# First values, keys and queries of a two-block layer side by side by k-tile, with squares by token and moving operands at multiples of 64 bytes

## The chip, the core and the metric

The kernel runs on one core of one Trainium2 chip. The metric is the device time of one execution in microseconds; three executions of the kernel before took 1695.17, 1696.14 and 1696.08 us, median 1696.08 us. A time is called "the same" here when it lies within 0.2% of the one before, about 3.4 us.

## The reference, cut

Two transformer blocks run one after the other on 256 tokens of 2048 features, all in float32. The change lies at the start of the first block; its second part (where tiles lie) touches all of both.

```python
def rmsnorm(x, g):
    y = xf * lax.rsqrt(jnp.mean(xf * xf, axis=-1, keepdims=True) + EPS)
    return (y * g.astype(jnp.float32)).astype(x.dtype)

def first_block(x, ...):
    h = rmsnorm(x, pre_mix_g[l])
    proj = h @ w_in[l]
    q_a, k_a, v_a, q_b, k_b, v_b, f_b = jnp.split(proj, cuts, axis=-1)
    o_a = swa_sink_attention(q_a, k_a, v_a, sinks[l])            # 16 heads of 64, 2 kv heads
    log_f = jax.nn.log_sigmoid(f_b + b_forget[l])
    o_b = forgetting_attention(q_b, k_b, v_b, log_f)             # 16 heads of 64
    mix = concat([rmsnorm(o_a), rmsnorm(o_b)]) @ w_out[l]
    x = x + rmsnorm(mix, post_mix_g[l])
    u = causal_dwconv(rmsnorm(x, pre_ffn_g[l]) @ w_up[l], ...)   # 2 x 5632 columns
    x = x + rmsnorm((gelu(gate) * val) @ w_down[l], post_ffn_g[l])
# then second_block(x, mem, ...): the products w_in_2, w_out_2, w_xq, w_xkv, w_xo
```

## The kernel before

Every projection is a product over 2048 features, that is 16 k-tiles of 128 (w_down has 44). Both operands are split into two float32r parts whose sum is the float32 value, so a product is three matmuls: high by high, high by low, low by high. Weights are loaded as raw blocks `wr` (4 buffers, on SyncE's queue, L76), the high part `wh` is made on ScalarE (L92), the low part `wl` on VectorE (L99), 3 buffers each.

A product has one of two forms. In **ws_sub** weights are stationary and the activations move: for each k-tile and each of two tiles of 128 output columns there is a pair, `wl` against 256 columns (L227) and `wh` against 512 columns (L228), the 512 being both parts of 256 tokens next to each other; the pair of the first k-tile stands at L224 and L225. An output group of 256 columns has 32 pairs at 16 k-tiles. In **as_chunk** activations are stationary and 388 to 414 columns of weights move, six matmuls per k-tile (L256 to L258).

TensorE, VectorE, ScalarE and GpSimd run in the order in which Python emits the work: projections are the main line, and generators (attention, norms) emit one stage at a time between k-tiles. In the first stage the order is: the 16 k-tiles of x (tile `R`) are loaded and split into tiles `X0` to `X3` (L193 on ScalarE, L201 on VectorE); the first chunk of 390 value columns runs over all 16 k-tiles; meanwhile the squares of x are made (two quarters on GpSimd at L530, two on ScalarE at L533), summed on GpSimd (L535, L536, L306), then by a matmul with ones (L292), and `rms` and `by_token` (L294 to L301, L313) give the scale by row (`rb1`, `rq`) and by token (`rb1c`). Then the chunk is evicted (L554), 128 columns of keys follow over all k-tiles, then four groups of windowed queries. The group of the queries called q0 below is the first of them, q1 the second.

A tile has a tag, and the tags' order of first use gives its place in SBUF. The places, read from the built program, as bytes modulo 64 within a partition (a moving operand of a pair starts at its tile's place plus a multiple of 2048 bytes):

```
tiles                                        before   after
X0 to X3  (activations, moving in pairs)       32       0
B3 B4 B7 B8 B9 B10 (the same, other stages)    32       0
B0 B1 B2 B5 B6 (the same)                       0       0
wh, wl (stationary in pairs, moving in chunks) 32      32
```

Before, the B tiles at 0 are all at a multiple of 128. After, X0 to X3, B6 and B7 are at 64 modulo 128, the other B tiles at 0. Of the pairs, 3104 of 3856 have their moving operand at 32 modulo 64 before, none after. In w_down an output group takes its 44 k-tiles in the order B0, B1, ... B10, four k-tiles (8 pairs) to a tile.

## Time and profile before

| what | value |
|---|---|
| median of three runs | 1696.08 us |
| span of the profiled execution | 1693.5 us |
| TensorE busy | 1642.7 us (97%) |
| TensorE weight loads busy | 1428.6 us (84%) |
| VectorE busy | 1133.0 us (67%) |
| ScalarE busy | 947.2 us (56%) |
| GpSimd busy | 390.8 us (23%) |
| mean of the DMA traffic | 178 GB/s |

The profile is of one execution; of it the span from the first to the last instruction is known, which is 2.6 us below the median of the three timed runs. Matmuls are pipelined and their ends are modelled, so "busy" of TensorE counts overlap and its mean per instruction says less than the distance from one start to the next.

### The profile page before, as it was taken

To read this page: it belongs to the slowest core of one execution; us is meant where nothing else is said; L and a number is where in the kernel's file an instruction comes from. 1 tells how busy PE (TensorE), PEld (TensorE's weight loads), DVE (VectorE), ACT (ScalarE), POOL (GpSimd) and SP (SyncE) were. 2 spreads that over 40 slices of the span, in tenths; PEclk is the share of its full clock that TensorE was granted. 3 is DMA by queue.
4 is the path that set the end of the run, shared out by engine and by line. 5 is a ranking of instruction groups with operands and counts; after the bars stand their busy time and mean duration, and the time that the engine had idled before them with its cause. 6 is when DMAs were issued, how large, how long until landed. Compare 5 with 4: busy or idle time off the path is not lost. (4 is left out here: it accounts for less than half of the span.)

```text
span 1693.5 us, 25090 instructions
## 1 busy us (share of the span) xinstructions
PE 1642.7 (97%) x9444; PEld 1428.6 (84%) x9444; DVE 1133.0 (67%) x1592; ACT 947.2 (56%) x1479; POOL 390.8 (23%) x300
## 2 busy tenths in 40 slices
PE   6999999989999999999999999997999999999996
PEld 6888888877888888888888888886989888888895
DVE  7677765788777777777775444468664555666766
ACT  5575566755555555555554444455445665655655
POOL 4434642343221122112210000003210222211112
PEclk9999999999999999999999999999999999999998
DMA  6545554745555555555555555664545544556752
GB/s 227 206 131 168 162 157 137 234 137 172 188 183 192 185 187 184 192 185 187 183 193 187 188 186 190 204 204 131 179 135 170 191 146 158 165 191 205 225 165 103
DMA packets 87465, 301.19 MB, mean 178 GB/s; under 512 B 9792, under 2 KB 9824, under 8 KB 87088
## 3 DMA queue, kind: packets, MB, share of 16 engines
q1 hardware_dynamic: 85968, 294.23, 53.2%
q0 software_dynamic: 1232, 5.08, 0.9%
q8 instruction: 74, 1.21, 0.3%
q14 instruction: 47, 0.39, 0.1%
q10 hardware_dynamic: 144, 0.28, 0.1%
HBM read 296.65 MB, written 2.90 MB: 177 GB/s over the span
## 5 line engine op out<-in xcount | busy, mean ns | idle before, releaser
L99 DVE TENSOR_TENSOR wl<-wr,wh 128x1024 fp32r<-128x1024 f32 (+5 forms) x556 | 709.6, 1278 | 328.7 <-ACT wh L92 327.8
L92 ACT ACTIVATE wh<-wr 128x1024 fp32r<-128x1024 f32 (+5 forms) x556 | 574.9, 1035 | 572.1 <-PE P L228 398.3
L228 PE MATMUL P<-X,wh 128*128 128x512 f32 x1867 | 664.0, 399 | 0.0
L228 PE MATMUL P<-B,wh 128*128 128x512 f32 x1734 | 617.3, 398 | 3.4 <-DVE B L201 3.3
L227 PE MATMUL P<-X,wl 128*128 128x256 f32 x1867 | 529.8, 284 | 1.3 <-ACT wh L92 1.3
L227 PE MATMUL P<-B,wl 128*128 128x256 f32 x1734 | 494.8, 285 | 8.9 <-DVE wl L99 8.9
L228 PEld LDWEIGHTS P<-X,wh 128*128 128x128 f32 x1867 | 352.6, 189 | 81.6
L228 PEld LDWEIGHTS P<-B,wh 128*128 128x128 f32 x1734 | 328.5, 189 | 79.4 <-DVE B L201 4.9
L227 PEld LDWEIGHTS P<-X,wl 128*128 128x128 f32 x1867 | 354.0, 190 | 6.9 <-issue 2.6
L227 PEld LDWEIGHTS P<-B,wl 128*128 128x128 f32 x1734 | 329.5, 190 | 13.6 <-DVE wl L99 10.1
L808 POOL TENSOR_TENSOR e<-e,rb 128x512 f32<-128x512 f32 x44 | 93.3, 2121 | 401.8 <-DVE e L273 395.3
L273 DVE TENSOR_TENSOR e<-P,e 128x512 f32<-128x512 f32 (+1 forms) x96 | 66.1, 688 | 147.1 <-ACT e L272 143.8
L330 POOL TENSOR_TENSOR acc<-acc,tc 128x512 f32<-128x512 f32 x18 | 26.9, 1497 | 274.8 <-ACT tc L329 274.8
L256 PE MATMUL P<-wh,B 128*128 128x412 f32 (+2 forms) x208 | 73.4, 353 | 0.0
L257 PE MATMUL P<-wl,B 128*128 128x412 f32 (+2 forms) x208 | 69.7, 335 | 1.0 <-DVE wl L99 1.0
L258 PE MATMUL P<-wh,B 128*128 128x412 f32 (+2 forms) x208 | 69.7, 335 | 0.0
L813 ACT ACTIVATE tc<-e,cols 128x256 f32<-128x256 f32 x88 | 48.2, 595 | 28.5 <-POOL e L808 28.5
L272 ACT ACTIVATE e<-P 128x512 f32<-128x512 f32 (+1 forms) x96 | 55.3, 577 | 0.0
L256 PE MATMUL P<-wh,X 128*128 128x390 f32 (+2 forms) x112 | 40.0, 357 | 7.4 <-ACT wh L92 7.4
L257 PE MATMUL P<-wl,X 128*128 128x390 f32 (+2 forms) x112 | 38.9, 347 | 6.0 <-DVE wl L99 6.0
L818 DVE SCALAR_TENSOR_TENSOR tc<-e,cols,tc 128x254 f32<-128x254 f32 x88 | 42.5, 483 | 3.1
L224 PE MATMUL P<-X,wh 128*128 128x512 f32 x117 | 43.6, 396 | 0.0
(287 smaller groups left out, 1621.4 us busy)
## 6 DMA issues: line engine op xcount, KB each, us to landing
wr<-w_up SPq DMA_DIRECT2D x176, 512.0 KB, 4.2
wr<-w_down SPq DMA_DIRECT2D x88, 512.0 KB, 4.4
wr<-w_out SPq DMA_DIRECT2D x64, 512.0 KB, 4.5
wr<-w_qkb SPq DMA_DIRECT2D x32, 512.0 KB, 3.9
wr<-w_sb SPq DMA_DIRECT2D x32, 512.0 KB, 4.0
wr<-w_gate SPq DMA_DIRECT2D x32, 512.0 KB, 3.9
wr<-w_v SPq DMA_DIRECT2D x24, 412.0 KB, 3.4
wr<-w_qa SPq DMA_DIRECT2D x16, 512.0 KB, 4.4
```

The lines of the kernel that those rows point to most:

```text
L92: k.nc.scalar.activation(h[:, :n], src, AF.Copy)
L99: self.k.nc.vector.tensor_tensor(out=l[:, :n], in0=src, in1=h[:, :n].bitcast(F32), op=ALU.subtract)
L224: mm(pt[t], h[:, o:o + P], xf, start=True, stop=False)
L227: mm(pt[t][:, 0:S], l[:, o:o + P], xk[:, 0, :], start=False, stop=False)
L228: mm(pt[t], h[:, o:o + P], xf, start=False, stop=last)
L256: mm(o, xh, hh, start=kt == 0, stop=False)
L257: mm(o, xh, ll, start=False, stop=False)
L258: mm(o, xl, hh, start=False, stop=kt == KT - 1)
L272: nc.scalar.activation(e1[:, t0:t1, :], p[:, 0:t1 - t0, S:2 * S], AF.Copy)
L273: nc.vector.tensor_tensor(out=e2[:, t0:t1, :], in0=p[:, 0:t1 - t0, 0:S], in1=e1[:, t0:t1, :], op=ALU.add)
L808: nc.gpsimd.tensor_tensor(out=e, in0=e, in1=self.rb2(self.r2), op=ALU.mult)
L813: nc.scalar.activation(y[:, t, :], e[:, t, :], AF.Identity, scale=w(t, 2), bias=w(t, 3))
```

## The change

Three things are done. **First**, the first 390 value columns, the 128 key columns and the 256 columns of q0 are laid side by side in one weight block per k-tile (`w_first`, 774 columns), and a loop over k-tiles does all three products of a k-tile before the next: 6 matmuls of the chunk, one pair of the keys, two pairs of q0, each into PSUM banks of its own. x is loaded in eight parts, two ahead of the loop and the rest within it, each k-tile is split two k-tiles ahead of its use, and the gains needed for that come in a small load of their own (`gain0`). **Second**, x is loaded a second time with tokens on partitions (`xtok`, two loads of 1 MB into tags B6 and B7), and ScalarE squares it and sums along the row in one instruction per half (`accum_out`). The scale by token comes from [128, 2] operands in `rms_tok`, the scale by row from a matmul of ones with a diagonal (`by_row`). The squares and sums on GpSimd are gone. **Third**, small pads (`pad`) and the new order of first use place the tiles as in the table above. From q1 on TensorE's order is as before, apart from five small transposes and sums of the forget gates, which stood among the keys and q0 and now stand in q1; the forget gates and the attention are started later by the generators' counts (2 and 8 k-tiles after q0).

The diff, cut to its core (the left out hunks remove comments, or rename a tag that nothing here rests on):

```diff
+    def pad(self, n=8):
+        self.uid += 1
+        self.nc.gpsimd.memset(self.sb.tile([P, n], F32, name=f"pad_{self.uid}", tag=f"pad{self.uid}", bufs=1), 0.0)
...
+    def ws_tiles(self, pt, xk, h, l, first, last):
+        mm = self.nc.tensor.matmul
+        xf = xk.rearrange("p a b -> p (a b)")
+        for t, o in enumerate(pt):
+            wh, wl = h[:, t * P:(t + 1) * P], l[:, t * P:(t + 1) * P]
+            if first:
+                mm(o, wh, xf, start=True, stop=False)
+                mm(o[:, 0:S], wl, xk[:, 0, :], start=False, stop=False)
+            else:
+                mm(o[:, 0:S], wl, xk[:, 0, :], start=False, stop=False)
+                mm(o, wh, xf, start=False, stop=last)
...
+    def as_halves(self, ps, xk, hh, ll, kt):
+        mm = self.nc.tensor.matmul
+        for half in range(2):
+            xh, xl = xk[:, 0, half * P:(half + 1) * P], xk[:, 1, half * P:(half + 1) * P]
+            o = ps[:, half, :hh.shape[1]]
+            mm(o, xh, hh, start=kt == 0, stop=False)
+            mm(o, xh, ll, start=False, stop=False)
+            mm(o, xl, hh, start=False, stop=kt == KT - 1)
...
+    def rms_tok(self, ssq, n, tag):
+        nc = self.nc
+        rc = self.t((P, 2), tag)
+        nc.scalar.activation(rc, ssq, AF.Ln, scale=1.0 / n, bias=self.epsc[:, 0:1])
+        nc.scalar.activation(rc, rc, AF.Exp, scale=-0.5)
+        m = self.t((P, 2), "rcm")
+        nc.vector.tensor_scalar(out=m, in0=ssq, scalar1=-0.5 / n, scalar2=-0.5 * EPS, op0=ALU.mult, op1=ALU.add)
+        for _ in range(2):
+            nc.vector.tensor_tensor(out=m, in0=m, in1=rc, op=ALU.mult)
+        nc.vector.scalar_tensor_tensor(out=rc, in0=m, scalar=1.5, in1=rc, op0=ALU.add, op1=ALU.mult)
+        dg = self.t((P, 2, P), "td", bufs=2)
+        for half in range(2):
+            nc.vector.tensor_scalar(out=dg[:, half, :], in0=self.ident, scalar1=rc[:, half:half + 1], scalar2=None,
+                                    op0=ALU.mult)
+        return rc, dg
+    def by_row(self, dg):
+        ps = self.p("O")
+        for half in range(2):
+            self.nc.tensor.matmul(ps[:, half * P:(half + 1) * P], self.ones, dg[:, half, :], start=True, stop=True)
+        return ps[:, 0:S]
...
+        self.gain0 = self.t((P, KT), "gain0")
+        nc.sync.dma_start(self.gain0, a["gain0"])
         nc.scalar.dma_start(self.cols, a["cols"])
         self.ident = self.t((P, P), "ident")
         nc.gpsimd.dma_start(self.ident, a["ident"])
         self.ones = self.t((P, P), "ones")
         nc.gpsimd.memset(self.ones, 1.0)
-        self.mhalf = self.t((P, 2), "mhalf")
-        nc.gpsimd.memset(self.mhalf, -0.5)
...
-        narrow("w_v", 0, V_CHUNKS)
-        wide("w_ka")
+        for i in range(KT):
+            units.append((a["w_first"][i], [FIRST_W]))
         wide("w_qa")
...
+        gain = lambda kt: self.gain0[:, kt:kt + 1]
+        def load(c):
             nc.sync.dma_start(R[:, 2 * c:2 * c + 2, :], a["xT"][:, 2 * c:2 * c + 2, :])
-            if c in (0, 2, 4):
-                self.ws.dma()
-        for kt in range(KT):
-            self.split(x(kt), R[:, kt, :], self.col("pre_mix", kt))
-            if kt in (1, 4, 7):
-                self.ws.split()
-                self.ws.flush()
-        acc = self.t((P, 2, 512), "B10")
-        accf = acc.rearrange("p a b -> p (a b)")
-        def squares():
-            for c in range(4):
-                src = R[:, 4 * c:4 * c + 4, :].rearrange("p a b -> p (a b)")
-                sq = self.t((P, 4 * S), f"B{c + 6}") if c else accf
-                if c < 2:
-                    nc.gpsimd.tensor_tensor(out=sq, in0=src, in1=src, op=ALU.mult)
-                else:
-                    yield 4
-                    nc.scalar.activation(sq, src, AF.Square)
-                if c:
-                    nc.gpsimd.tensor_tensor(out=accf, in0=accf, in1=sq, op=ALU.add)
-            nc.gpsimd.tensor_tensor(out=acc[:, 0, :], in0=acc[:, 0, :], in1=acc[:, 1, :], op=ALU.add)
-            yield 10
-            yield from self.first_norm([self.fold(acc[:, 0, :].rearrange("p (a b) -> p a b", a=2))])
+        for c in range(2):
+            load(c)
+            self.ws.dma()
+            self.ws.dma()
+        xt = [self.t((P, D), tg) for tg in ("B6", "B7")]
+        self.pad()
+        ssq = self.t((P, 2), "ssq")
+        sq = self.t((P, D), "B10")
 
         V = [self.t((P, D), "B3"), self.t((P, D), "B4")]
+        self.pad()
         o = VW + 16
         ka = V[0][:, o:o + S]
         acca = [V[0][:, o + i * S:o + (i + 1) * S] for i in (1, 2)]
         accb = [V[1][:, o + P + i * S:o + P + (i + 1) * S] for i in (0, 1)]
...
-        def v_chunk(ci):
+        def v_evac(ps, ci):
             c0, c1 = V_CHUNKS[ci]
-            if ci == 0:
-                it = self.push(squares())
-            ps = self.as_chunk(x, c1 - c0)
-            if ci == 0:
-                self.drain(it)
             for half in range(2):
                 nc.scalar.activation(V[half][:, c0:c1], ps[:, half, :c1 - c0], AF.Copy, scale=self.rc[:, half:half + 1])
 
-        v_chunk(0)
-        rb, rq = self.rb, self.rq
-        fg = self.push(self.fox_gates(V), 2)
+        def v_chunk(ci):
+            v_evac(self.as_chunk(x, V_CHUNKS[ci][1] - V_CHUNKS[ci][0]), ci)
         va = lambda h, half: V[half][:, (h // 8) * 64:(h // 8) * 64 + 64]
         vb = lambda h, half: V[half][:, 144 + h * 64:144 + h * 64 + 64]
 
-        ps = self.big()
-        for k0 in (0, 8):
-            self.ws_sub(ps, x, list(range(k0, k0 + 8)), (0, KT - 1), 1)
-        self.push(self.scaled(ps, ka.unsqueeze(1), rb))
+        n = V_CHUNKS[0][1]
+        psv, psq, psk = self.big(), self.big(), self.p("S", bufs=2)
+        for kt in range(-2, KT):
+            i = kt + 2
+            if i < KT:
+                self.split(x(i), R[:, i, :], gain(i))
+                if i % 2 and i // 2 + 2 < 8:
+                    load(i // 2 + 2)
+                if i in (8, 10):
+                    nc.sync.dma_start(xt[i // 2 - 4], a["xtok"][:, i // 2 - 4, :])
+            self.ws.split()
+            self.ws.flush()
+            if kt < 0:
+                continue
+            h, l, m = self.ws.get()
+            xk = x(kt)
+            self.as_halves(psv, xk, h[:, :n], l[:, :n], kt)
+            for pt, o in (([psk], n), ([psq[:, t, :] for t in range(2)], n + P)):
+                self.ws_tiles(pt, xk, h[:, o:o + len(pt) * P], l[:, o:o + len(pt) * P], kt == 0, kt == KT - 1)
+            self.ws.done()
+            if kt in (10, 12):
+                half = kt // 2 - 5
+                nc.scalar.activation(sq, xt[half], AF.Square, accum_out=ssq[:, half:half + 1])
+            if kt == 13:
+                self.rc, dg = self.rms_tok(ssq, D, "rb1c")
+        ps = self.by_row(dg)
+        self.rb, self.rq = self.t((P, S), "rb1"), self.t((P, S), "rq")
+        nc.vector.tensor_copy(self.rb, ps)
+        nc.vector.tensor_scalar(out=self.rq, in0=ps, scalar1=0.125, scalar2=None, op0=ALU.mult)
+        rb, rq = self.rb, self.rq
+        v_evac(psv, 0)
+        self.push(self.scaled([psk], ka.unsqueeze(1), rb))
...
-            ps = self.ws_group(x)
+            ps = self.ws_group(x) if g else psq
             self.push(self.scaled(ps, qa[:, 2 * g:2 * g + 2, :], rq, "swa", 4))
             if g == 0:
+                fg = self.push(self.fox_gates(V), 2)
                 side = self.push(chain(
                     self.attn64(order, qf, kf, va, self.alibi, sink, lambda: oa, acca, pts_a, 5, "swa"),
-                    self.group_norm_split(oa, acca, 0, dst), fox()), 4)
+                    self.group_norm_split(oa, acca, 0, dst), fox()), 8)
...
+    A["xtok"] = np.ascontiguousarray(x.reshape(2, P, D).transpose(1, 0, 2))
...
+    A["w_first"] = _groups(w, [np.concatenate([vcols[:V_CHUNKS[0][1]], _r(1024, 1152), qa[0]])], 1)
+    A["w_qa"] = _groups(w, qa[1:])
```

TensorE at the end of the first k-tile: `wh0`, `wl0` are the parts of the first weight block, `P` and `S` are PSUM tiles. Before:

```order
L256 MATMUL P_17_155<-wh0_99,X0_8_77 128x390
L257 MATMUL P_17_155<-wl0_100,X0_8_77 128x390
L258 MATMUL P_17_155<-wh0_99,X0_8_77 128x390
L256 MATMUL P_17_155<-wh1_113,X0_8_77 128x390
L257 MATMUL P_17_155<-wl1_114,X0_8_77 128x390
L258 MATMUL P_17_155<-wh1_113,X0_8_77 128x390
```

After (the lines have moved: L255 to L257 is the chunk, L223 to L227 the pairs):

```order
L255 MATMUL P_20_101<-wh0_106,X0_8_77 128x390
L256 MATMUL P_20_101<-wl0_107,X0_8_77 128x390
L257 MATMUL P_20_101<-wh0_106,X0_8_77 128x390
L223 MATMUL S_22_103<-X0_8_77,wh0_106 128x512
L224 MATMUL S_22_103<-X0_8_77,wl0_107 128x256
L223 MATMUL P_21_102<-X0_8_77,wh0_106 128x512
L224 MATMUL P_21_102<-X0_8_77,wl0_107 128x256
```

What moved: the pair of the keys (`S_22`) and the two pairs of q0 (`P_21`, of which the first is shown), which stood behind all 16 k-tiles of the chunk, now stand behind each k-tile's six matmuls, and the chunk's matmuls of `wh1` follow them.

TensorE at the end of that stage, before (`P_25` are the keys, `wh7` the last block of the chunk):

```order
L256 MATMUL P_17_155<-wh7_246,X3_11_80 128x390
L257 MATMUL P_17_155<-wl7_247,X3_11_80 128x390
L258 MATMUL P_17_155<-wh7_246,X3_11_80 128x390
L313 MATMUL O_22_317<-ones_3_68,rb1_20_279 128x1 x2
L224 MATMUL P_25_326<-X0_8_77,wh8_264 128x512
L225 MATMUL P_25_326<-X0_8_77,wl8_265 128x256
```

After (`P_21` with `wh15` is the last pair of q0, `P_41` is q1, `td` holds the diagonals):

```order
L226 MATMUL P_21_102<-X3_11_80,wl15_393 128x256
L227 MATMUL P_21_102<-X3_11_80,wh15_392 128x512
L349 MATMUL O_26_457<-td_25_418,ones_4_70 128x128 x2
L223 MATMUL P_41_483<-X0_8_77,wh16_421 128x512
L224 MATMUL P_41_483<-X0_8_77,wl16_422 128x256
```

What moved: behind the last k-tile stand the two matmuls of `by_row` and then at once q1; the keys and q0 are done.

GpSimd behind its loads of constants, before (`B10` collects the squares, `R` is x):

```order
L530 TENSOR_TENSOR B10_12_147<-R_7_76 128x1024
L530 TENSOR_TENSOR B7_15_151<-R_7_76 128x1024
L535 TENSOR_TENSOR B10_12_147<-B10_12_147,B7_15_151 128x1024
L535 TENSOR_TENSOR B10_12_147<-B10_12_147,B8_16_154 128x1024
L535 TENSOR_TENSOR B10_12_147<-B10_12_147,B9_18_182 128x1024
L536 TENSOR_TENSOR B10_12_147<-B10_12_147 128x512
L306 TENSOR_TENSOR B10_12_147<-B10_12_147 128x256
L281 TENSOR_TENSOR B3_13_148<-e2_31_383,rb1_20_279 128x256
```

After:

```order
L152 MEMSET pad_14_93 128x8
L152 MEMSET pad_19_99 128x8
L152 MEMSET pad_31_470 128x8
L290 ISA
L290 TENSOR_TENSOR B3_17_97<-e2_30_467,rb1_27_460 128x256
L290 TENSOR_TENSOR B0_32_472<-e2_40_480,rq_28_461 128x512
```

What moved: the squares and their sums are gone from GpSimd; its first operation on data is the scaling of the keys. On ScalarE the squares stand as two instructions of 2048 columns between the splits of k-tiles 12 to 15.

## Rows read from the trace of the kernel before

**Rows 1.** The page: its first line.

```profile
span 1693.5 us, 25090 instructions
```

**Rows 2.** Who waited for whom on TensorE: us, times, longest.

```profile
PE P L256 <- ACT wh L92: 7.4, 1, 7.4
PE P L257 <- DVE wl L99: 7.1, 4, 3.4
```

**Rows 3.** Windows: length, busy of PE, PEld, DVE, ACT, POOL, PEclk, DMA, GB/s.

```profile
7.37:12.20 4.83, 4.52 (x13) 4.04 (x13) 4.83 (x4) 3.65 (x8) 4.39 (x2) 1.00 1.04 394
12.20:15.88 3.68, 0.28 (x3) 0.01 (x1) 3.68 (x3) 3.68 (x9) 2.71 (x2) 0.96 0.81 311
15.88:19.00 3.12, 3.12 (x10) 3.12 (x11) 3.12 (x6) 1.83 (x3) 1.14 (x1) 0.50 0.51 135
19.00:24.13 5.13, 2.81 (x16) 2.48 (x14) 5.13 (x9) 2.66 (x3) 2.05 (x2) 1.00 0.23 74
```

**Rows 4.** Timeline of the first stage: start, duration, engine, line.

```profile
7.35 0.97 DVE L99 TENSOR_TENSOR wl<-wr,wh 128x780 fp32r<-128x780 f32 x1 [0.38 <-ACT wh L92]
...
7.37 0.69 PE L256 MATMUL P<-wh,X 128*128 128x390 f32 x1 [7.37 <-ACT wh L92]
...
12.58 2.41 POOL L535 TENSOR_TENSOR B<-B,B 128x1024 f32<-128x1024 f32 x1
12.71 3.11 DVE L99 TENSOR_TENSOR wl<-wr,wh 128x780 fp32r<-128x780 f32 x1
...
15.88 0.69 PE L257 MATMUL P<-wl,X 128*128 128x390 f32 x1 [3.40 <-DVE wl L99]
...
24.59 0.34 PE L256 MATMUL P<-wh,X 128*128 128x390 f32 x1
...
24.77 0.34 PE L257 MATMUL P<-wl,X 128*128 128x390 f32 x1
```

**Rows 5.** Groups on ScalarE, 0 to 40 us: busy us, mean ns.

```profile
L193 ACT ACTIVATE X<-R,cols 128x256 fp32r<-128x256 f32 x16 | 6.9, 495 | 3.9 <-DMA cols<-cols 3.5 <-DMA R<-xT 0.5
L92 ACT ACTIVATE wh<-wr 128x780 fp32r<-128x780 f32 x8 | 6.8, 854 | 8.0 <-PE P L258 7.3 <-DMA wr<-w_v 0.7
...
L533 ACT ACTIVATE B<-R 128x1024 f32<-128x1024 f32 x2 | 2.1, 1039 | 0.0
```

**Rows 6.** Groups on VectorE, 0 to 40 us.

```profile
L201 DVE SCALAR_TENSOR_TENSOR X<-R,cols,X 128x256 fp32r<-128x256 f32 x16 | 12.1, 813 | 6.1 <-ACT X L193 6.1
L99 DVE TENSOR_TENSOR wl<-wr,wh 128x780 fp32r<-128x780 f32 x8 | 10.9, 1381 | 2.3 <-ACT wh L92 2.3
```

**Rows 7.** Timeline of TensorE where q1 starts.

```profile
53.61 0.40 PE L224 MATMUL P<-X,wh 128*128 128x512 f32 x1
```

**Rows 8.** The page: costliest groups, the 512 column matmul of a pair.

```profile
L228 PE MATMUL P<-X,wh 128*128 128x512 f32 x1867 | 664.0, 399 | 0.0
L228 PE MATMUL P<-B,wh 128*128 128x512 f32 x1734 | 617.3, 398 | 3.4 <-DVE B L201 3.3
```

**Rows 9.** Timeline of TensorE over one output group of w_down.

```profile
978.84 0.39 PE L224 MATMUL P<-B,wh 128*128 128x512 f32 x1
...
987.17 0.28 PE L227 MATMUL P<-B,wl 128*128 128x256 f32 x1
...
998.39 0.28 PE L227 MATMUL P<-B,wl 128*128 128x256 f32 x1
...
1009.69 0.39 PE L224 MATMUL P<-B,wh 128*128 128x512 f32 x1
```

**Rows 10.** Windows of two output groups of w_up, TensorE alone.

```profile
412.41:423.52 11.11, 11.11 (x66) 1.00 0.54 177
434.81:446.09 11.28, 11.28 (x65) 1.00 0.56 187
```

**Rows 11.** Windows of four k-tiles each of a chunk of w_in_2: B5, then B9.

```profile
1190.05:1194.61 4.56, 4.56 (x25) 1.00 0.81 248
1194.61:1199.11 4.50, 4.50 (x25) 1.00 0.84 301
```

More of the change, by code (lines that the diff above doesn't have):

```diff
@@ L43 @@
 V_CHUNKS = [(0, 390), (390, 780), (780, 1168)]
+FIRST_W = 390 + P + 2 * P
 V2_CHUNKS = [(0, 414), (414, 828), (828, 1240), (1240, 1652), (1652, 2064)]
@@ L207, in split @@
         self.split_l(dst, src, g)
+    def ws_tiles(self, pt, xk, h, l, first, last):
[9 more added lines that the diff above has]
+                mm(o, wh, xf, start=False, stop=last)
     def ws_sub(self, ps, x, kts, nk, ntile=2):
-        mm = self.nc.tensor.matmul
         h, l, n = self.ws.get()
@@ L217, in ws_sub @@
         for j, kt in enumerate(kts):
-            xk = x(kt)
-            xf = xk.rearrange("p a b -> p (a b)")
-            first, last = kt == nk[0], kt == nk[1]
-            for t in range(ntile):
-                o = j * w + t * P
-                if first:
-                    mm(pt[t], h[:, o:o + P], xf, start=True, stop=False)
-                    mm(pt[t][:, 0:S], l[:, o:o + P], xk[:, 0, :], start=False, stop=False)
-                else:
-                    mm(pt[t][:, 0:S], l[:, o:o + P], xk[:, 0, :], start=False, stop=False)
-                    mm(pt[t], h[:, o:o + P], xf, start=False, stop=last)
+            self.ws_tiles(pt, x(kt), h[:, j * w:(j + 1) * w], l[:, j * w:(j + 1) * w], kt == nk[0], kt == nk[1])
             if j == len(kts) - 1:
@@ L240, in ws_group @@
         return ps
+    def as_halves(self, ps, xk, hh, ll, kt):
[6 more added lines that the diff above has]
+            mm(o, xl, hh, start=False, stop=kt == KT - 1)
     def as_chunk(self, x, n):
-        mm = self.nc.tensor.matmul
         ps = self.big()
@@ L250, in as_chunk @@
             for j in range(per):
-                xk = x(kt)
-                hh, ll = h[:, j * n:(j + 1) * n], l[:, j * n:(j + 1) * n]
-                for half in range(2):
-                    xh, xl = xk[:, 0, half * P:(half + 1) * P], xk[:, 1, half * P:(half + 1) * P]
-                    o = ps[:, half, :n]
-                    mm(o, xh, hh, start=kt == 0, stop=False)
-                    mm(o, xh, ll, start=False, stop=False)
-                    mm(o, xl, hh, start=False, stop=kt == KT - 1)
+                self.as_halves(ps, x(kt), h[:, j * n:(j + 1) * n], l[:, j * n:(j + 1) * n], kt)
                 if j == per - 1:
@@ L1115, in sgu @@
         r = self.t((P, 4), "sr")
+        mhalf = self.t((P, 2), "fe")
+        nc.gpsimd.memset(mhalf, -0.5)
         vs = [V[half][:, 512:1024] for half in range(2)]
@@ L1126, in sgu @@
         nc.gpsimd.tensor_scalar(out=r[:, 0:2], in0=r[:, 0:2], scalar1=1.0 / 512, scalar2=EPS, op0=ALU.mult, op1=ALU.add)
-        nc.gpsimd.tensor_tensor(out=r[:, 2:4], in0=r[:, 0:2], in1=self.mhalf, op=ALU.pow)
+        nc.gpsimd.tensor_tensor(out=r[:, 2:4], in0=r[:, 0:2], in1=mhalf, op=ALU.pow)
         yield 5
@@ L1334, in _layout @@
     A["w_v"] = vu
[L1335 to L1338 removed]
+    qa = [np.concatenate([_r(64 * j, 64 * j + 64), _r(64 * j + 512, 64 * j + 576),
+                          _r(64 * j + 64, 64 * j + 128), _r(64 * j + 576, 64 * j + 640)]) for j in (0, 2, 4, 6)]
+    A["w_first"] = _groups(w, [np.concatenate([vcols[:V_CHUNKS[0][1]], _r(1024, 1152), qa[0]])], 1)
+    A["w_qa"] = _groups(w, qa[1:])
     g = []
```

14 lines of the change are left out of this document (5 added, 9 removed).

## The prediction

> **What bounds the kernel now.** I read the head of the page first, for the span against which the sum is made: 1693.5 us [rows 1], 2.6 us under the median of the runs. TensorE is busy nearly all of it, so only two things can move the time: stretches in which it waits or runs at its low clock, and the distance between its matmuls where it never waits. The change touches both. The list of who waited for whom shows, for TensorE, two waits that lie in the first stage: 7.4 us before its first matmul and 7.1 us for weights' low parts, the longest 3.4 us [rows 2].
>
> Next, the first stage in windows, from the first matmul at 7.37 us to the start of q1 at 53.61 us [rows 4, 7]: 46.24 us. In it TensorE's busy time falls short of the windows by 4.83 - 4.52, 3.68 - 0.28 and 5.13 - 2.81, together 6.0 us [rows 3]. It also runs at its low level, 1.2 instead of 2.4 GHz: from 15.88 to 19.00 the granted clock is 0.50, which costs half of 3.12, 1.6 us; and from 7.37 to 12.20, where 13 matmuls took 4.52 us, 0.35 us each, against 0.18 us from one start to the next later [rows 3, 4]. The 1.00 printed for that window can't be its clock, so it costs another 2.3 us. About 9.9 us of the 46.24 are no work.
>
> The timeline says why TensorE waits until 15.88 us: the low part it needs is one VectorE subtraction that took 3.11 us, beside a GpSimd sum of squares from 12.58 us; the same subtraction took 0.97 us earlier [rows 4]. Over the stage VectorE's subtraction has a mean of 1381 ns and the split of x 813 ns [rows 6]. So it is GpSimd's squares that hold VectorE, and with it TensorE; DMA isn't short (394 GB/s while it is wanted, 74 GB/s later) [rows 3].
>
> Last, the steady stages. The page gives 399 ns for the 512-column matmul from X and 398 ns from B [rows 8], as if place didn't matter. But its ends are modelled, and B mixes both places; starts are the better measure. In one output group of w_down, counted by order, B0 to B2 (at 0 modulo 64) take from 978.84 to 987.17, 24 pairs, 347.1 ns a pair; B7 to B10 (at 32) take from 998.39 to 1009.69, 32 pairs, 353.1 ns [rows 9]. All eight groups repeat this. In w_up all tiles lie at 32, and its groups come at two paces: 11.11 us for 32 pairs and 11.28 us [rows 10]. Of 44 groups two, back to back up to 423.52 us, go at the faster pace, the others at the slower. So a place at 32 allows the slow pace and does not force it; a place at 0 modulo 64 never shows it.
>
> **The first stage, step by step.** The loop has per k-tile six chunk matmuls at 0.18 us [rows 4] and three pairs at 0.347 us, 2.12 us, over 16 k-tiles 33.9 us. Its start: gains no longer ride on the large load, ScalarE splits one k-tile less before the first weights, but one more small load is issued ahead; I leave the first matmul at 7.4 us. The second waits for `wl0` as now, some 0.7 us. The low clock then costs some 2 us, since TensorE is busy from about the same moment; it fell again only after the idle 3.40 us, which the loop hasn't. 7.4 + 0.7 + 33.9 + 2 + 0.5 for `by_row` and the PSUM gives q1 at 44.5 us, 9.1 us earlier. The forget gates' five small matmuls, among the keys and q0 before, now come later and cost some 0.9 us there: net gain **8.2 us**.
>
> What must hide beneath 2.12 us per k-tile: ScalarE, 0.495 for x and 0.854 for the weights, 1.35 us, and two squares of 2048 columns at twice 1.04 us [rows 5], which fit into the lead of two k-tiles. VectorE, by its means with GpSimd running, 0.813 + 1.381 = 2.19 us [rows 6], just too slow: 16 times 0.07 us, 1.1 us lost; by 0.97 and half a microsecond without GpSimd, 1.5 us, hidden. GpSimd now does nothing there, so I take the second. DMA: 0.53 MB per k-tile, and 2.1 MB of `xtok` over about four k-tiles, 4.2 MB in 8.5 us, which at 394 GB/s [rows 3] needs 10.7 us; four raw buffers cover the 2.2 us. If not, PE waits those 2.2 us. On SyncE's queue the raw blocks and x's last two parts stand behind the two `xtok` loads, and x's parts 2 to 7 behind raw loads that wait for VectorE to free a buffer; each part is issued some three k-tiles, 6 us, ahead of its split. Behind a square that waited for `xtok` stand ScalarE's splits of the next k-tile, two k-tiles ahead of their use. At the loop's end q1 needs the PSUM of the chunk; behind the chunk's last matmul come six of keys and q0, 1.04 us, while ScalarE evicts twice 390 columns, each between the 0.495 us of 256 and the 0.854 us of 780 [rows 5]: a wait of 0 to 0.7 us, within the 0.5 above.
>
> A rule of the Trainium skill bears on VectorE here: "SBUF — State Buffer", section "SBUF: two separate sides", says that VectorE and GpSimd share a port pair held exclusively for a whole instruction. The 3.11 us against 0.97 us [rows 4] agree; by the rule alone VectorE's load would be the 1.5 us and the sum the same.
>
> **The places.** 3104 pairs move from 32 to 0 modulo 64; 48 lie in the first stage and gain nothing, since it ran at the fast pace. Of the rest about nine in ten go at the slow pace (42 of w_up's 44 groups, all of w_down's tiles at 32). The price of a pair: 353.1 - 347.1 = 6.0 ns in w_down [rows 9]; 0.17 us over 32 pairs, 5.3 ns, in w_up [rows 10]. I take 5.8 ns, for 3056 x 0.92 pairs: **16.3 us**; bounds 3056 x 0.85 x 5.3 = 13.8 and 3056 x 6.0 = 18.3. These stages have no slack elsewhere to lose: TensorE's busy time fills both windows of rows 10.
>
> One cost goes the other way. In chunks the stationary activations move from 32 to 0 too, while the moving weights stay at 32. Four k-tiles with stationary B5, at 0, took 4.56 us and with B9, at 32, 4.50 us [rows 11]: 2.5 ns a matmul. Some 740 matmuls change: 0 to 1.9 us, I take **1.0 us**.
>
> Sum, against the profiled span: 1693.5 - 8.2 - 16.3 + 1.0 = 1670.0, and with the 2.6 us around it **1672.6 us**.
>
> A rule of the Trainium skill speaks against this part: "SBUF — State Buffer", section "Specifications (TRN2)", gives cachelines of 16 bytes and a penalty per line crossed; 32 and 0 modulo 64 both start such a line, so by it the places change nothing and the sum would be 1687.9 us. The trace disagrees in w_down, where nothing but the tile changes in the middle of a group [rows 9].
>
> **Rivals.** *The places give nothing* (a): the slow pace belongs to something else that goes with low addresses, or with the order of tiles. For it: X at 32 runs fast in the first stage and in two groups of w_up. Against it: tiles at 0 show no slow stretch in eight groups. 1696.1 - 8.2 = 1688 us. *64 modulo 128 isn't enough* (b): before, every fast tile was at 0 modulo 128, and X0 to X3 come to lie at 64. Then 2000 of 3104 pairs, 10.5 of the 16.3 us, gain nothing, and B6's 80 pairs lose 0.5 us: 1672.6 + 11.0 = 1683.6 us. The 6.0 ns are near one more 64-byte piece of a 2048-byte row (a 32nd of 213 ns, 6.7 ns, at 2.4 GHz), half of what a 128-byte piece would give, which speaks for 64. *The first stage gains nothing* (c): VectorE or loads hold the loop, TensorE idles and falls to 1.2 GHz once or twice; at (33.9 + 8.2) / 16 = 2.63 us a k-tile nothing is left of the 8.2 us: 1672.6 + 8.2 = 1680.8 us. *Slower* (d): the loop is held so that TensorE idles in every k-tile and stays at 1.2 GHz throughout. Twice 2.12 us is 4.24 us a k-tile, 67.8 us for the loop, 33.9 us more of which 2 are counted already: 1672.6 + 31.9 = 1704.5 us. It decides from (33.9 + 8.2 + 16.3 - 1.0) / 16 = 3.59 us a k-tile. Against it: for that the supply of 0.53 MB would have to fall to 148 GB/s, under two fifths of what rows 3 show, or VectorE's 2.19 us to grow by two thirds without GpSimd beside it.
>
> **How the numbers follow.** Forecast 0.70, (a) 0.09, (b) 0.10, (c) 0.08, (d) 0.03. The forecast's own range: the first stage from 3.3 us less (VectorE's 1.1 and the loads' 2.2) to 1 us more, the places 13.8 to 18.3, the chunks 0 to 1.9, so 1668.6 to 1679.3 us; down to 1666 if the loop's 2 us at the low clock shrink as well. 1666 to 1684 takes in (c) and half of (b) and leaves out (a) and (d): some 0.81. A measurement tells 0.2%, 3.4 us, from no change. All cases but (d) are faster; with a small share of (a) and (c) worse than reckoned: faster 0.95, same 0.02, slower 0.03. Predicted: **1672.6 us**, from 1666 to 1684.
>
> **What would show it.** TensorE's first wait of 3.40 us gone, no granted clock of 0.50 between 15 and 20 us, q1's first matmul at 44 to 45 us, VectorE's subtraction near 1 us in the loop. In w_up every group at 11.1 us, in w_down all tiles alike at 347 ns a pair. The chunks of w_in_2 a little longer. The prediction is wrong if w_up's groups still take 11.28 us (a or b; B7 to B10 in w_down then tell them apart), or if TensorE waits within the loop (c).

## The result, and the profile after

The changed kernel takes 1680.91 us (median of four runs, 1680.15 to 1682.2) against 1695.62 us for the kernel before on the same chip: a ratio of 0.9918, 95% interval 0.9904 to 0.9932. The forecast was 1672.6 us, so of the 23.5 us expected 14.7 came. The time lies inside the stated range, in its upper part. The profiled execution's span:

```profile
span 1678.5 us, 25107 instructions
```

The first stage in windows over all engines (columns as in [rows 3]), from the first matmul to q1's first at 46.06 us, and VectorE's two groups in it:

```profile
8.32:14.00 5.68, 5.37 (x15) 4.68 (x16) 4.03 (x7) 3.68 (x7) 0.00 (x0) 1.00 0.95 335
14.00:46.06 32.06, 32.06 (x183) 30.03 (x182) 20.21 (x33) 22.10 (x35) 0.00 (x0) 1.00 0.83 289
```

```profile
L100 DVE TENSOR_TENSOR wl<-wr,wh 128x774 fp32r<-128x774 f32 (+1 forms) x18 | 17.8, 995 | 12.1 <-ACT wh L93 12.1
L207 DVE SCALAR_TENSOR_TENSOR X<-R,gain,X 128x256 fp32r<-128x256 f32 x16 | 7.7, 481 | 8.9 <-ACT X L199 8.9
```

From 14.00 us on TensorE is never idle: 32.06 of 32.06 us. VectorE's subtraction has fallen from 1381 to 995 ns (two of the 18 have 1024 columns) and the split of x from 813 to 481 ns [rows 6], and VectorE now waits for ScalarE. The loop does what was forecast; it only starts 0.95 us later (first matmul at 8.32, not 7.37 us).

Behind it TensorE's windows show what was not forecast. q1 starts at 46.06 us, q2 at 63.82 us:

```profile
46.06:51.87 5.81, 5.81 (x35) 1.00 0.62 213
51.87:53.50 1.63, 0.00 (x1) 1.00 0.38 118
53.50:55.10 1.60, 1.60 (x14) 1.00 0.53 207
55.10:58.51 3.41, 3.41 (x13) 0.50 0.44 154
58.51:63.82 5.31, 5.31 (x37) 1.00 0.40 137
```

Here the columns are window and length, TensorE's busy time, its granted clock, DMA share and GB/s. In q1 TensorE stands still for 1.63 us and soon after runs 3.41 us at the 1.2 GHz level. The timeline names what it waited for, the forget gates:

```profile
53.50 0.40 PE L691 MATMUL T<-fz,cp 128*128 128x16 f32 x2 [1.63 <-DVE fz L687]
```

Then the paces. Two output groups of w_up, as in [rows 10]:

```profile
429.90:441.00 11.10, 11.10 (x65) 1.00 0.53 191
441.00:452.10 11.10, 11.10 (x65) 1.00 0.54 185
```

All groups of w_up but the two at its start are like these. One output group of w_down, 966.29 to 997.05 us, took 30.85 us in [rows 9]; then four of its tiles, eight pairs each: B1, B7, B8, B9:

```profile
966.29:997.05 30.76, 30.76 (x178) 1.00 0.55 189
```

```profile
969.10:971.90 2.80, 2.80 (x17) 1.00 0.35 110
985.85:988.62 2.77, 2.77 (x17) 1.00 0.54 195
988.62:991.46 2.84, 2.84 (x17) 1.00 0.54 189
991.46:994.26 2.80, 2.80 (x17) 1.00 0.53 192
```

Only B7 goes at the fast pace, 2.77 us or 346.6 ns a pair. B1, B8 and B9 are at 0 modulo 64 too and take 2.80 and 2.84 us. Counted from the start of one pair to the start of the next, over all groups, the six tiles B0, B1, B2, B5, B8 and B9 settle at 350.0 ns, and B0 to B2 were fast before. These six, which lie behind the weights' buffers, are called the tail tiles below. The chunk of [rows 11], B5 and B9:

```profile
1175.51:1180.03 4.52, 4.52 (x26) 1.00 0.79 241
1180.03:1184.54 4.51, 4.51 (x26) 1.00 0.88 305
```

The ledger, from the starts of the same matmuls in both traces (after less before, us; the column on the right is what the terms of the prediction come to by stage, the places' term by the pairs at 32 modulo 64 that each stage had before, rounded):

```
stretch                                    measured   forecast
up to q1's first matmul                      -7.55      -9.1
q1 and q2 (30.55 before, 34.25 after)        +3.70      +0.6
rest of w_in, w_out, w_xk                    -0.78   \
w_in_2's groups                              -0.84    > -5.8 together
w_out_2                                      +0.50   /
w_up                                         -7.74      -7.5
w_down                                       -0.63      -2.0
w_in_2's start and chunks                    -1.79      +0.7
last products and end                        +0.14      -0.3
span                                        -15.0      -23.5
```

### The profile page after: what moved, and what is told of

Its sections match the earlier page's. It is cut to its first block, busy times and chain, and to the rows that moved or that the text cites. A ratio compares the mean times of both kernels' runs of the same rounds, so it can differ in the third digit from the quotient of the medians.

```text
span 1678.5 us, 25107 instructions
## 1 busy us (share of the span) xinstructions
PE 1631.0 (97%) x9442; PEld 1425.9 (85%) x9442; DVE 1126.9 (67%) x1596; ACT 947.7 (56%) x1483; POOL 371.8 (22%) x296
## 5 line engine op out<-in xcount | busy, mean ns | idle before, releaser
L227 PE MATMUL P<-X,wh 128*128 128x512 f32 x1852 | 651.3, 394 | 0.0
L227 PE MATMUL P<-B,wh 128*128 128x512 f32 x1734 | 615.1, 396 | 2.7 <-DVE B L207 2.6
L226 PE MATMUL P<-X,wl 128*128 128x256 f32 x1852 | 524.3, 283 | 1.3 <-ACT wh L93 1.3
L227 PEld LDWEIGHTS P<-X,wh 128*128 128x128 f32 x1852 | 349.8, 189 | 74.2
L227 PEld LDWEIGHTS P<-B,wh 128*128 128x128 f32 x1734 | 327.7, 189 | 77.9 <-DVE B L207 4.5
L226 PEld LDWEIGHTS P<-X,wl 128*128 128x128 f32 x1852 | 349.9, 189 | 6.6 <-issue 2.5
L282 DVE TENSOR_TENSOR e<-P,e 128x512 f32<-128x512 f32 x95 | 65.7, 691 | 141.7 <-ACT e L281 137.6
L255 PE MATMUL P<-wh,B 128*128 128x412 f32 (+2 forms) x208 | 73.2, 352 | 0.0
L257 PE MATMUL P<-wh,B 128*128 128x412 f32 (+2 forms) x208 | 69.5, 334 | 0.0
L281 ACT ACTIVATE e<-P 128x512 f32<-128x512 f32 x95 | 55.0, 579 | 1.7 <-DVE e L282 1.7
L255 PE MATMUL P<-wh,X 128*128 128x390 f32 (+2 forms) x112 | 39.3, 351 | 8.3 <-ACT wh L93 8.3
L223 PE MATMUL P<-X,wh 128*128 128x512 f32 x116 | 43.9, 400 | 0.0
L363 POOL TENSOR_TENSOR B<-B,tc 128x512 f32<-128x512 f32 x14 | 22.0, 1571 | 89.8 <-ACT tc L362 89.8
```

Of the source, the lines that this page charges most:

```text
L226: mm(o[:, 0:S], wl, xk[:, 0, :], start=False, stop=False)
L227: mm(o, wh, xf, start=False, stop=last)
L255: mm(o, xh, hh, start=kt == 0, stop=False)
L257: mm(o, xl, hh, start=False, stop=kt == KT - 1)
L281: nc.scalar.activation(e1[:, t0:t1, :], p[:, 0:t1 - t0, S:2 * S], AF.Copy)
L282: nc.vector.tensor_tensor(out=e2[:, t0:t1, :], in0=p[:, 0:t1 - t0, 0:S], in1=e1[:, t0:t1, :], op=ALU.add)
```

## The experiments

In the sketches of edits, `pad(n)` moves all that is allocated behind it by 4n bytes. Runs with a time but no ratio were executed once; they are read by their traces, not by their times.

**Are places the cause at all?** e1 puts every moving tile at 32 modulo 64 and keeps the rest of the change.

```diff
+        self.pad()
         X = [self.t((P, 4, 2, S), f"X{i}", F32R) for i in range(4)]
...
         V = [self.t((P, D), "B3"), self.t((P, D), "B4")]
-        self.pad()
...
-        self.pad()
+        self.pad(16)
         qa = self.t((P, 8, S), "B0")
```

> The changed kernel with every moving activation tile shifted by 32 bytes, so that all lie at 32 modulo 64 again; the order of the first stage and the squares stay as changed, wh and wl stay at 32. Theory (the place of the moving operand sets the pace of a pair): w_up's groups of 32 pairs go back from 11.10 to 11.28 us, 44 times 0.185, 8 us, and w_in, w_out and w_down add 2 to 5 us: 10 to 13 us slower than the changed kernel, some 1691 to 1694 us, and only 2 to 5 us under the kernel before, which is what the first stage alone is then worth. Rival (the pace comes from the order of first use or from what else the change moved): w_up's groups stay at 11.10 us and the time stays within 2 us of the changed kernel's.

Measured: 1694.03 us, ratio to before 1.0001 (0.9991 to 1.0011). A group of w_up:

```profile
511.75:523.04 11.29, 11.29 (x67) 1.00 0.56 188
```

So where the tiles lie is the cause of w_up's gain. In this trace, of an execution that took 2.3 us more than the median, the first part, up to q3, is 2.5 us shorter than before, and the rest of the span 3.6 us longer: among it 1.0 at w_in_2's start and 1.5 in the groups of w_in_2 and w_out_2, some of whose tiles were fast before.

**Is it a multiple of a power of two?** e3 spreads the six tail tiles; e4 puts X at multiples of 512 and 2048.

```diff
         qa = self.t((P, 8, S), "B0")
+        self.pad(16)
         oa = self.t((P, 8, S), "B5")
...
+        self.pad(112)
         ohl = [self.t((P, 4, 2, S), tg, F32R) for tg in ("B9", "B10")]
...
+        for tg in ("fz", "fe", "fc"):
+            nc.gpsimd.memset(self.t((P, 2, 16), tg), 0.0)
+        self.pad(32)
         ring_a = self.t((P, 5, 3 * P), "B8")
...
+        self.pad(32)
         qb = self.t((P, 8, S), "B1")
```

> The changed kernel with the six tiles behind the work tiles spread: B0 stays at a multiple of 2048 bytes, B5 comes to 64 modulo 2048, B9 to 512, B8 to 1024, B1 and B2 to 1152 (128 modulo 1024). In the changed kernel all six lie at multiples of 2048 and their pairs in w_down take 350 ns, while B3, B4, B6, B7, B10 take 346.6 to 347. Theory (a moving operand at a multiple of a larger power of two has a slower pace): B5, B1 and B2 fall to 346.6 ns; if the power is 512, B9 and B8 stay at 350; if it is 1024, only B8 stays with B0; if 2048, B0 alone stays. Rival (these tiles are slow because they lie behind the weights' buffers, or because of their turn in the group): all six stay at 350 ns wherever they lie. By the theory the whole is 1 to 3 us faster, by the rival the same.

Measured: 1682.15 us (one run). Windows of B2, B5, B8 and B9 in one group of w_down:

```profile
971.74:974.51 2.77, 2.77 (x17) 1.00 0.66 222
980.06:982.84 2.78, 2.78 (x18) 1.00 0.58 197
988.38:991.18 2.80, 2.80 (x17) 1.00 0.57 193
991.18:993.98 2.80, 2.80 (x17) 1.00 0.58 199
```

B2 (128 modulo 512) and B5 (64) have become fast, B8 (1024) and B9 (512) have not. Taken alone this fits the theory with a power of 512.

```diff
-        X = [self.t((P, 4, 2, S), f"X{i}", F32R) for i in range(4)]
+        self.pad(48)
+        X = [self.t((P, 4, 2, S), f"X{i}", F32R) for i in range(2)]
+        self.pad(128)
+        X += [self.t((P, 4, 2, S), f"X{i}", F32R) for i in range(2, 4)]
```

> The changed kernel with X0 and X1 at multiples of 2048 bytes and X2 and X3 at 512 modulo 2048; behind them everything moves on, so that the six tail tiles lie at 704 modulo 2048 (64 modulo 128). Theory (multiples of a large power of two are slow): w_up's pairs with X0 and X1 take 350 instead of 346.7 ns, so its groups take 11.15 us if 512 is free of it and 11.21 us if 512 is slow too, against 11.10; 2.4 to 4.8 us are lost over 44 groups, and w_down gains 1 to 2 us, since its tail tiles fall to 346.6 ns. Rival (the tail tiles are slow for another reason than their place modulo a power of two): w_up's groups stay at 11.10 us, and the tail tiles stay at 350 ns.

Measured: 1682.34 us (one run). A group of w_up, then B1 and B9 in one group of w_down:

```profile
498.57:509.67 11.10, 11.10 (x66) 1.00 0.57 187
971.17:973.97 2.80, 2.80 (x17) 1.00 0.36 111
993.53:996.33 2.80, 2.80 (x17) 1.00 0.59 192
```

All of w_up stays at 346.7 ns a pair with X0 and X1 at multiples of 2048, and the tail tiles, now at 64 modulo 128, still take 350.0. Both expectations of the theory fell. What e4 left alone is the distance between the tail tiles and the weight buffers, all moved by the same 704 bytes; what e3 changed is that distance, for B1, B2 and B5 modulo 256. Before, `wl` and `wh` lay at 352 modulo 512 with all slow tiles at 352 and all fast ones at 256: there, too, distance says what place had seemed to say.

**Distance or place?** A distance is here the place of a pair's moving tile less that of `wl`, modulo 256 bytes; but for e10, that to `wh` is the same. In the changed kernel it is 160 for X, B6 and B7, 224 for B3, B4 and B10, and 96 for the tail tiles. e5 moves only the weight buffers by 32 bytes, e6 weights and activations together.

```diff
         V = [self.t((P, D), "B3"), self.t((P, D), "B4")]
-        self.pad()
+        self.pad(16)
...
-        self.pad()
         qa = self.t((P, 8, S), "B0")
```

> The changed kernel with wh and wl moved by 32 bytes, from 32 to 0 modulo 64; every moving tile stays where it is. With the runs so far two theories of the pace stand. Theory D (the distance from a pair's moving tile to its weight tile decides: a multiple of 64 is slow, 32 modulo 64 fast, except +96 modulo 256, which the tail tiles have in the changed kernel and in the run with X at 2048): X is now at distance -128, B3, B4 and B10 at -64, the tail tiles at +64, all multiples of 64, so w_up's groups take about 11.28 us again instead of 11.10 and the whole 8 to 12 us more, 1689 to 1693 us. Theory M (the moving tile's own place modulo 64 decides, as the prediction had it): nothing changes in w_up, 11.10 us, and the time stays within 2 us of the changed kernel's; in chunks stationary and moving are then both at 0, which by the prediction's third term gives back up to 1.9 us.

Measured: 1690.34 us, ratio 0.9975 (0.9963 to 0.9986). No moving tile was touched, and w_up is slow again:

```profile
508.60:519.83 11.23, 11.23 (x67) 1.00 0.55 187
```

```diff
+        self.pad()
         X = [self.t((P, 4, 2, S), f"X{i}", F32R) for i in range(4)]
```

> The changed kernel with everything from X on moved by 32 bytes, the weights and all moving tiles alike: moving tiles at 32 modulo 64, wh and wl at 0. Theory D (distance): every distance is that of the changed kernel, so w_up's groups take 11.10 us, the tail tiles 350 ns a pair in w_down and B4, B6, B7 346.7, and the time is that of the changed kernel, 1681 us, within 2 us. Theory M (place of the moving tile): all moving tiles are at 32, so w_up's groups take 11.28 us and the time is that of the run with the places put back, some 12 us more.

Measured: 1680.47 us, ratio 0.9916 (0.9901 to 0.9931), the changed kernel's. Every moving tile lies at 32 modulo 64, and a group of w_up, then B1, B7 and B9 in w_down, take what they take in the changed kernel:

```profile
507.25:518.36 11.11, 11.11 (x67) 1.00 0.56 191
```

```profile
968.41:971.21 2.80, 2.80 (x17) 1.00 0.36 107
985.15:987.93 2.78, 2.78 (x18) 1.00 0.54 189
990.77:993.57 2.80, 2.80 (x17) 1.00 0.59 192
```

The moving tile's own place decides nothing; its distance from the weights does.

**Which distances, and from which weight tile?** e9 tries three more distances on the tail tiles; e10 moves `wl` alone.

```diff
-        self.pad()
+        self.pad(56)
         qa = self.t((P, 8, S), "B0")
...
+        self.pad(16)
         ohl = [self.t((P, 4, 2, S), tg, F32R) for tg in ("B9", "B10")]
...
+        self.pad(48)
         qb = self.t((P, 8, S), "B1")
```

> The changed kernel with the tail tiles at three other distances from wh and wl: B0 and B5 at +32 modulo 256 (192 modulo 512), B9 and B8 at +96 modulo 256 (256 modulo 512), B1 and B2 at +32 modulo 512. So far pairs were fast at distances of 160 and 224 modulo 256 and took 350 ns at 96. Theory D with a period of 256 bytes: B9 and B8 still take 350 ns; with a period of 512 they become fast. For +32 nothing was seen yet: by the rule of the odd multiples of 32 it is fast, 346.7; by likeness to +96 (the weight tile below the moving one by less than 128 bytes) it is slow, 350. In w_down the time follows: between no gain and 1.5 us less over its eight groups.

Measured: 1680.33 us (one run). Windows of B2 (+32), B4 (not moved, +224), B8 and B9 (+96):

```profile
972.82:975.59 2.77, 2.77 (x17) 1.00 0.63 195
978.40:981.23 2.83, 2.83 (x18) 1.00 0.67 221
989.55:992.39 2.84, 2.84 (x17) 1.00 0.62 201
992.39:995.19 2.80, 2.80 (x17) 1.00 0.58 187
```

+32 is fast; +96 stays slow at another multiple of 256, so the period is not 512 bytes; 256 fits all runs. And a surprise: B4, whose place and distance did not change, went from 2.77 to 2.83 us; what changed are the tiles around it.

```diff
         h = k.sb.tile([P, 1024], F32R, name=f"wh{i}", tag="wh", bufs=self.AHEAD)
+        if i == 0:
+            k.pad()
...
-        self.pad()
         qa = self.t((P, 8, S), "B0")
```

> The changed kernel with wl alone moved by 32 bytes to 0 modulo 64; wh and all moving tiles stay. For X the distance to wh stays -96, the one to wl becomes -128. If the slow pace comes from the moving tile against wl (its load lies beside the 512 column matmul of the pair before), w_up's groups take 11.2 to 11.28 us as in the run with both moved; if it comes from wh (loaded beside the 256 column matmul, when weight loads and matmul are nearly equally long), they stay at 11.10 us. If it takes both, a time between is seen. Theory M (the moving tile's own place), already unlikely, says 11.10 us.

Measured: 1689.22 us (one run). A group of w_up:

```profile
508.68:519.90 11.22, 11.22 (x66) 1.00 0.56 189
```

It is as slow as with both moved, so for X the distance to `wl` is enough. B3, B4 and B10, at -64 from `wl` and -32 from `wh`, settle at 346.7 ns in this run, though, which -64 from both (e5) did not; that it is `wl` alone in every case is not shown. All distances seen, as moving tile less `wl` modulo 256, with the pace counted from starts where a tile has settled (e10, with two distances at once, is left out):

```
distance   ns a pair        where
  0        353, some 346.7  before (X, B3, B4, B7 to B10); e1 (B3, B4; B10 fast)
 32        346.7            e9 (B0, B1, B2, B5)
 64        349 to 355       e5 (six tail tiles)
 96        350.0            after (six tail tiles), e3, e4, e6, e9
128        349 to 352       e1 (six tail tiles), e5 (X)
160        346.7            before (B0 to B2, B6; B5 350.0 over its eight pairs); after (X, B6, B7); e3, e4, e6, e9, e11
192        353.3            e1 (X), e5 (B3, B4)
224        346.7 or 353.3   after (B3, B4, B10), e3, e4, e6; slow in e9 (B3, B4)
```

**What did the first stage's gain go to?** e2 moves the gates' matmuls 4 k-tiles later (`yield 6` to `yield 10` behind the gates' arithmetic).

> The changed kernel, but the forget gates' matmuls come 10 instead of 6 k-tiles behind the arithmetic that feeds them. Theory (the first stage's gain was given back in q1, where TensorE waited 1.63 us for the gates and then ran 3.41 us at half clock because of that idle time): the wait at 51.9 us is gone, no granted clock of 0.50 near 55 us, q2 starts 3.3 us earlier, and the whole is 3.3 us faster, 1677.6 us. Rival A (the low clock there has another cause): only 1.6 us are gained. Rival B (another wait takes its place, the scores' first matmul for the scaled queries): nothing is gained.

Measured: 1682.49 us, ratio 0.9938 (0.9923 to 0.9953). The wait at the gates and the low clock in q1 are gone, but q3 starts at 80.33 us, as in the changed kernel (80.31). TensorE's waits, and GpSimd's rows beside them:

```profile
61.21 0.55 PE L398 MATMUL T<-ident,sm 128*128 128x128 f32 x3 [1.66 <-DVE acc L701]
69.92 0.93 PE L439 MATMUL S<-B,B 64*128 64x128 f32 x8 [2.26 <-POOL B L290]
```

```profile
61.44 0.58 POOL L703 DMA_DIRECT2D negc<-acc  x1 [2.73 <-DMA wr<-w_qa]
64.74 1.10 POOL L707 DMA_DIRECT2D B<-negc  x2 [2.72 <-ACT B L401]
...
68.60 1.26 POOL L290 TENSOR_TENSOR B<-e,rq 128x512 f32<-128x512 f32 x1
```

Rival B came true: the scaling of q1 (L290) stands in GpSimd's queue behind the write and the read back of the gates, and the scores' matmul waits for it. Before, these two DMAs were issued at 46.2 and 49.2 us, ahead of q1.

e7 starts the gates at once and puts `yield 4` between the two DMAs.

> The changed kernel with the forget gates' arithmetic started at once with q1 instead of 2 k-tiles later, ahead of a VectorE subtraction of 2.33 us in its queue, and with the DMA that reads the gates back 4 k-tiles behind the one that writes them, so that GpSimd doesn't stand still for the landing. Theory (the first stage's gain was given back through the gates' new place): the 1.63 us wait at 51.9 us is gone, with it the low clock behind it, no other wait comes up in q1 and q2, and the stretch from q1 to the end of q2, 34.3 us in the changed kernel and 30.6 us before, comes to 31 to 31.5 us; the whole is 2.5 to 3.5 us faster than the changed kernel. Rival (as with the later gates: GpSimd's queue, in which the scaling of q1 stands behind bias and gates, holds the scores in any case): the stretch stays at 34 us, with the wait at another place.

Measured: 1680.64 us, ratio 0.992 (0.9903 to 0.9936). q1 and q2 take 32.69 us, between the theory and its rival: 1.6 less than in the changed kernel, with two shorter waits and no low clock; of the 3.7 us, 2.1 stay, and the timed gain is too small to be measured:

```profile
51.15 0.40 PE L691 MATMUL T<-fz,cp 128*128 128x16 f32 x2 [0.68 <-DVE fz L687]
68.33 0.93 PE L439 MATMUL S<-B,B 64*128 64x128 f32 x8 [0.78 <-POOL B L290]
```

**Were GpSimd's squares the old first stage's trouble?** e8 gives GpSimd work of that kind beside the new loop; nothing reads its results.

```diff
+            if kt in (2, 3):
+                half = kt - 2
+                nc.gpsimd.tensor_tensor(out=V[half][:, 0:1024], in0=R[...], in1=R[...], op=ALU.mult)
+            if kt == 4:
+                for _ in range(3):
+                    nc.gpsimd.tensor_tensor(out=V[0][:, 0:1024], in0=V[0][:, 0:1024], in1=V[1][:, 0:1024], op=ALU.add)
```

> The changed kernel, with two products of 1024 columns and three sums of 1024 columns given to GpSimd beside the first loop, from its third k-tile on; nothing reads their results. Theory (it was GpSimd's squares that held VectorE's subtraction and so TensorE in the first stage): while they run, some 12 us, the subtraction of 774 columns takes 2 to 3 us instead of 0.97, VectorE needs more than the 2.15 us that TensorE takes per k-tile, and q1 starts 4 to 8 us later than at 46.1 us. Rival (the wait came from the loads, or from what else the old first stage had in its queues): the subtraction stays near 1 us, and q1 starts within 1 us of 46.1 us.

Measured: 1685.55 us (one run). The pair of q1 that starts at 46.49 us in the changed kernel starts at 52.57:

```profile
21.18 8.03 POOL L605 TENSOR_TENSOR B<-B,B 128x1024 f32<-128x1024 f32 x3
21.30 3.17 DVE L100 TENSOR_TENSOR wl<-wr,wh 128x774 fp32r<-128x774 f32 x1
24.39 2.62 DVE L207 SCALAR_TENSOR_TENSOR X<-R,gain,X 128x256 fp32r<-128x256 f32 x1
...
30.09 0.69 PE L256 MATMUL P<-wl,X 128*128 128x390 f32 x1 [3.18 <-DVE wl L100]
```

The subtraction takes 3.17 us beside GpSimd's sums, TensorE waits 3.18 us for the next one, and its clock falls to 0.51 right behind (29.60 to 33.10 us). These are the rows of [rows 4] again, so the cause is shown. The Trainium skill's rule in "SBUF — State Buffer", section "SBUF: two separate sides", of a port pair that VectorE and GpSimd share, agrees with both.

**A version that is faster than both.** e11 puts all moving tiles at +160 from the weights and takes e7's gates, with two k-tiles more ahead of their matmuls; e12 is the changed kernel beside it.

```diff
-        self.pad()
-        ssq = self.t((P, 2), "ssq")
         sq = self.t((P, D), "B10")
...
         V = [self.t((P, D), "B3"), self.t((P, D), "B4")]
-        self.pad()
+        ssq = self.t((P, 2), "ssq")
+        self.pad(16)
...
-        self.pad()
+        self.pad(24)
         qa = self.t((P, 8, S), "B0")
...
```

> The changed kernel with every moving tile at +160 modulo 256 from wl and wh (B10, B3 and B4 go back by 64 bytes, the six tail tiles forward by 64), and with the forget gates started at once with q1, their matmuls 8 k-tiles later, and the read back of the gates 4 k-tiles behind its write. Theory D: all tiles of w_down take 346.7 ns a pair, with no step at the borders between tiles; against the changed kernel w_down gains some 1.7 us, w_in_2, w_out_2 and the last products 1.5 to 2 us together. The gates: q1 and q2 take 31 to 32 us instead of 34.3, 2 to 3 us. Together 5 to 6 us faster than the changed kernel, a span of 1673 us, 1675 us timed. Rival (the places hold only for X, and what the tail gains is lost in chunks or in waits): 1679 to 1681 us.

> The changed kernel itself, beside the run with all tiles at +160, on the same chip, so that the two can be compared: 1681 us, a ratio of 0.992 to the kernel before.

Measured: e11 1676.55 us, ratio to before 0.9897 (0.9883 to 0.9911); e12 1681.31 us, 0.9929 (0.9915 to 0.9942). e11 is 4.8 us faster than the changed kernel. A group of w_down, and TensorE's one wait in q1 and q2:

```profile
964.27:994.78 30.51, 30.51 (x177) 1.00 0.60 189
```

```profile
68.93 1.06 PE L439 MATMUL S<-B,B 64*128 64x128 f32 x8 [2.00 <-POOL B L290]
```

Counted from starts, each of the eleven tiles of w_down takes 346.6 to 346.8 ns a pair, without a step at the borders; 88 pairs of 346.7 ns are 30.51 us. The gates' half of the edit gave nothing: q1 and q2 take 34.42 us, with the wait for GpSimd in place of the one for the gates.

## Why the prediction came out as it did

**The loop: right.** The first wait of 3.40 us and the low clock behind it are gone, the subtraction is at 0.97 us, TensorE never waits from 14 us on, and e8 brings the old trouble back by GpSimd's work alone. q1 came at 46.06 instead of 44.5 us: 0.95 us of it is the first matmul, 0.6 us that the matmuls kept to half pace until 14 us. The first matmul's start varied between 6.9 and 9.1 us over all runs, so it is no firm loss.

**The step that failed in the first stage** is "the forget gates' five small matmuls ... now come later and cost some 0.9 us there". The matmuls themselves do; but what feeds them was moved too: VectorE's and ScalarE's small operations behind a subtraction of 2.33 us, and two DMAs in GpSimd's queue ahead of the scaling that the scores need. The subtraction itself stood beside a GpSimd operation, the scaling of q0; one of the same size took 1.22 us at 45.55 us. This resembles [rows 4], though no run tests it here:

```profile
49.40 1.30 POOL L290 TENSOR_TENSOR B<-e,rq 128x512 f32<-128x512 f32 x1 [0.81 <-DVE e L282]
49.44 2.33 DVE L100 TENSOR_TENSOR wl<-wr,wh 128x1024 fp32r<-128x1024 f32 x1
```

The stretch grew by 3.7 us: 1.63 of waiting, 1.7 by the low clock behind it (half of 3.41), the rest the matmuls. Net, the first stage was worth 3.85 us by q3 instead of 8.2. This split holds for the profiled execution alone. Ten profiles have these gates; in all of them TensorE waits for the gates, 1.61 to 2.01 us, in eight the low clock follows, for 3.4 or 6.8 us, and q1 and q2 take 33.9 to 36.3 us. In e10 and e12 no low clock follows, and yet e12, the changed kernel once more, takes 33.90 us, with a second wait, for GpSimd's scaling of q1:

```profile
69.25 0.93 PE L439 MATMUL S<-B,B 64*128 64x128 f32 x8 [0.77 <-POOL B L290]
```

So without the low clock most of its 1.7 us would have been lost all the same: e12's stretch is 0.35 us shorter. e2 and e11 show that moving the gates within q1 only moves the wait to GpSimd; e7's gain, 1.2 to 1.6 us against e12 and the changed kernel's first profile, is seen in its trace, not in its time.

**The places: w_up's term right by number, its cause wrong.** That "a place at 0 modulo 64 never shows" the slow pace was the failing step. The trace of before already spoke against it: in the output group of [rows 9] B5, at 0 modulo 64, takes 350.0 ns a pair, three more than B0 to B2, behind the slow B4:

```profile
992.82:995.62 2.80, 2.80 (x18) 1.00 0.58 195
```

e5 and e6 show that the tile's own place has no part in it. The Trainium skill's 16-byte cachelines ("SBUF — State Buffer", section "Specifications (TRN2)"), by which 32 and 0 should be alike, thus agree with e6 (1680.47 us), but say nothing of the distance that does the work. w_up's 7.74 us against 7.5 came because the change, moving X and the weights to other places, also changed their distance from 0 to 160. That it fell on a fast one was luck: at 128 (e5) and 192 (e1) X is slow. For the same reason w_down gave 0.63 instead of 2.0 us: six tiles came to +96, four of which had been at 160; and w_out_2 lost 0.5 us.

**The places: the other stages mis-sized.** 6.7 of the 16.3 us were reckoned for w_in, w_out, w_in_2, w_out_2 and the last products, by the share of slow pairs in w_up and w_down. In the trace of before the pairs of w_in and w_out average 350.6 and 350.5 ns, not 353. With all tiles fast, in e11, these stages from q3 on, without w_in_2's start and chunks, give 2.7 us against before (0.5 in w_in from q3 on, 0.8 in w_out, 1.0 in w_in_2's groups, 0.2 in w_out_2, 0.1 behind it).

**The chunks: sign not borne out.** The term of +1.0 us rested on 4.56 against 4.50 us; after, the two tiles take 4.52 and 4.51. The stretch's -1.79 us goes with where the low clock fell: before in two pieces (1155.6 to 1159.0 and 1179.5 to 1182.9 us), after in one from 1140.5 to 1147.4 us, among waits of TensorE. The other runs have between -1.9 and +1.0 us there: -1.1 to -1.9 with one piece, -0.6 to +1.0 with two. So a term of 1 us can't be read from this stretch.

**The rivals.** (a) was right that something other than the place sets the pace, and wrong that the change would gain nothing by it. (b) fell: X at 64 modulo 128 is fast. (c)'s time, 1680.8 us, is nearly the measured one, by accident and not for its reason: the loop was not held, half of its gain was lost behind it. (d) did not come near.

## What to carry to other kernels

Where matmuls run without waiting, their pace can still depend on the distance between the moving tile and the weight tiles: count starts tile by tile, and try a pad of 32 bytes on one of the two. When two causes fit the same places, move one party at a time: e5 and e6 settled in two runs what no reading of the first trace could, since there place and distance went together. When a step is moved, follow every queue that feeds it, not just the instructions on the engine that is full.
